# Eight plain feed-forward tiles for six, the factor and modulation sums moved beside them, and a last stage that begins on six output tiles

## The chip, the cores and the metric

The kernel runs on one core of a Trainium2 chip. The metric is the device time in microseconds. Before the change three runs gave 1978.41, 1980.34 and 1980.6, median 1980.34.

## The reference

One layer of a streaming encoder, for 1024 prompt frames and 64 sample frames (1088 tokens in all), model width 1024. Only the last third of the kernel is changed; it computes this:

```
mod = (silu(c) @ w_ada + b_ada).reshape(B, 6, D_MODEL)
sh_m, sc_m, gt_m, sh_f, sc_f, gt_f = (mod[:, j] for j in range(6))
...
u = _rmsnorm(x, g_pre_ffn) * (1.0 + sc_f) + sh_f
f = (jax.nn.silu(u @ w_ffn_gate) * (u @ w_ffn_up)) @ w_ffn_down
x = x + gt_f * _rmsnorm(f, g_post_ffn)
```

The hidden width is 2816, that is 22 tiles of 128 features. `gt_f`, the last sixth of `mod`, is needed only at the very end.

## The kernel before, in words

Every product is done in float32r with each operand split into a high and a low part, so that one product becomes three matmuls (high times high, low weight times high, high weight times low). Weights come from HBM in pieces of 128x512 on SP's queue; ScalarE rounds a piece to its high part (`wh`, line 159) and VectorE subtracts to get the low part (`wl`, line 163). All matmuls are issued at line 132.

The order of the work on each engine is fixed when the program is built. A small model of the machine (`Sched`) keeps a clock per engine; side jobs are Python generators that are resumed between matmuls when the modelled time has come, and what they issue then lands at that place in each engine's queue. Within one engine the order stays as issued.

The feed-forward part has three stages.

1. Plain tiles (`f_tile`): for a feature tile, gate and up products over three chunks of 364, 364 and 360 tokens, each product 24 matmuls into one of three PSUM banks of the tag `d`. ScalarE applies silu to the gate bank, VectorE multiplies by the up bank and forms the low part (tile `hst`), and the result is stored to `d_h` in HBM by a DMA on POOL's queue. Here `NPLAIN` = 6 tiles.
2. Pairs (`gu_pair`): the other 16 tiles are taken two at a time, with Winograd's form of Strassen's method: 7 half-size products (`STEPS`) in place of 8, for gate and then up, and for two halves of the tokens, p = 0 and p = 1, of 2x272 tokens each. A pair is 2x7x2 groups of 12 matmuls of 272 columns. The token side enters as itself (`b11`, `b21`, `b22`) and as four sums `t1` to `t4`, the right factors (`rh`, `rl`), which `right_factors(p)` forms on VectorE and ScalarE, one k index after another. The weight sums (`ws`) are formed on VectorE in scratch slots. Results are gathered in `g[p]`. At the end of a pair `store` takes the high part `hh`, subtracts it from `g[p]` in place, and sends both to `d_h` with two DMAs; the next pair's first gate step writes `g[p]` again.
3. Down (`down_order`): 8 output tiles for three chunks of 416, 416 and 256 tokens; operands `ho` come back from `d_h`. The first chunk begins with three output tiles side by side, so that the weights and operands are taken k range by k range; the others go one tile at a time. `y_chain` then normalises, multiplies by `gt_f` times the gain (`ggf`) and adds the residual.

`ada_rest(3)` forms `gt_f`: 16 loads of 128x512 of `w_ada` on POOL's queue into two halves of one slot, two VectorE accumulations each (`adac`, lines 167 and 172), then a few float32 matmuls into `ps_ms`. It is spawned when the last stage begins. `right_factors(0)` is spawned with the sixth plain job, `right_factors(1)` after it.

Large tiles live in an arena of 39 slots that are handed out first in, first out.

Of the kernel before, what the change touches and what calls it, by code (L numbers as in the profile page):

```python
# [11 lines left out]
F32 = mybir.dt.float32  # L12
F32R = mybir.dt.float32r
AF = mybir.ActivationFunctionType
OP = mybir.AluOpType
# [19 lines left out]
YCH = [(0, 416), (416, 832), (832, T)]  # L35
YSEG = [[(0, 416, 0)], [(0, 416, 0)], [(0, TP - 832, 0), (TP - 832, T - 832, 1)]]
NF = DFF // P
NPLAIN = 6
DNK = [(0, 4), (4, 8), (8, 12), (12, 16), (16, 20), (20, 22)]
HALF = 272  # L40
PAIRS = (0, 2 * HALF)
# [188 lines left out]
def f32(ap):  # L230
    return ap.bitcast(F32)
# [3 lines left out]
def hybrid_step(ctx: ExitStack, tc: tile.TileContext, io):  # L235
    nc = tc.nc
    S = Sched(nc)
# [6 lines left out]
    A = Arena(arena_pool, NSLOT)  # L244
# [5 lines left out]
    def ps(tag, cols=512):  # L250
        cnt[0] += 1
        return psum.tile([P, cols], F32, name=f"ps_{tag}{cnt[0]}", tag=tag, bufs=CAP[tag])
# [42 lines left out]
    class Stream:  # L295
# [37 lines left out]
        def source(self, kind, r, m):  # L333

            if kind is None:
                t, tm = self.raw[r]
                return t[:, 0:m], tm, 1
            (a11, t0), (a21, t1), (a12, t2), (a22, t3) = self.raw[r:r + 4]
            a11, a21, a12, a22 = (x[:, 0:m] for x in (a11, a21, a12, a22))
            if self.sums is None:  # L340
                two = [A.get("ws", F32, [2, 512]) for _ in range(2)]
                self.sum_slots = two
                self.sums = [two[i // 2][:, i % 2, :] for i in range(4)]
            s1, s2, s3, s4 = (x[:, 0:m] for x in self.sums)
            if kind == "11":
                return a11, t0, 0
            if kind == "12":
                return a12, t2, 0
            if kind == "22":
                return a22, t3, 1  # L350
            if kind == "s1":
                return s1, S.tt(s1, a21, a22, OP.add, after=max(t1, t3)), 0
            if kind == "s2":
                return s2, S.tt(s2, s1, a11, OP.add), 0
            if kind == "s3":
                return s3, S.tt(s3, a21, a11, OP.add), 2
            return s4, S.tt(s4, s2, a12, OP.add, after=t2), 1
# [60 lines left out]
    W = Stream()  # L418
# [31 lines left out]
    def down_order(c):  # L450

        if c == 0:
            yield from (((0, 1, 2), a, b) for a, b in DNK)
        for m in range(0 if c else 3, 8):
            yield from (((m,), a, b) for a, b in DNK)

    plain_jobs = [(0, (0,)), (1, (0,)), (0, (1,)), (1, (1,)), (2, (0, 1)), (3, (0, 1)), (0, (2,)), (1, (2,)), (2, (2,)),
# [381 lines left out]
    for c, (c0, c1) in enumerate(CH):  # L839
        for i in range(2):  # L840
            p = kps[i, c]
            n = c1 - c0 if c < 2 else 296
            t = S.now + 0.1
# [61 lines left out]
    for tt in range(9):  # L905
# [4 lines left out]
        p = ps(("po", "ms", "d")[min(tt, 2)])  # L910
        a, m = (tt * P, P) if tt < 8 else (TP, TS)
# [11 lines left out]
        t = S.now + 0.1  # L923
        f = S.act(vs[s][0:m, r, :], p[0:m, 0:256], AF.Copy, after=t)
# [197 lines left out]
    for kind, j in order_a2:  # L1122
        w = W.use()
        if kind == "q":
            q2 = [A.get("q", F32R) for _ in range(2)]
            for c0, c1 in CH:
                p = dense(w, u, c0, c1)
                n = c1 - c0
# [410 lines left out]
    def right_factors(p):  # L1539

        b0 = PAIRS[p]
        rec = A.get("rec", F32, [2, 2 * HALF])
        tf = A.get("tf", F32, [4, HALF])

        def calm():
            while S.t["dve"] > S.now + 0.3:
                yield max(S.now + 0.1, S.t["dve"] - 0.2)

        for i in range(4):
            while len(A.free) < 5:  # L1550
                yield S.now + 0.5
            hi, lo = A.get("rh", F32R, [4, HALF]), A.get("rl", F32R, [4, HALF])
            yield from calm()
            for j, k in enumerate((i, i + 4)):
                S.tt(rec[:, j, :], f32(u2[k][0][:, b0:b0 + 2 * HALF]), f32(u2[k][1][:, b0:b0 + 2 * HALF]), OP.add)
            b11, b12, b21, b22 = (rec[:, j, h * HALF:(h + 1) * HALF] for j in range(2) for h in range(2))
            t1, t2, t3, t4 = (tf[:, j, :] for j in range(4))
            yield from calm()
            S.tt(t1, b11, b12, OP.subtract)
            S.stt(t2, t1, -1.0, b22, OP.mult, OP.subtract)  # L1560
            S.tt(t3, b22, b12, OP.subtract)
            f = S.stt(t4, t2, -1.0, b21, OP.mult, OP.subtract)
            f = S.act(hi[:, :, :], tf[:, :, :], AF.Copy, after=f)
            yield f
            yield from calm()
            S.tt(lo[:, :, :], tf[:, :, :], f32(hi[:, :, :]), OP.subtract, after=f)
            right[p][i] = (hi, lo)
        rec.free()
        tf.free()

    def factor(p, i, name):

        b0 = PAIRS[p]
        if name[0] == "b":
            k = i + 4 * (name[1] == "2")
            h = int(name[2]) - 1
            return tuple(u2[k][l][:, b0 + h * HALF:b0 + (h + 1) * HALF] for l in range(2))
        j = int(name[1]) - 1
        return tuple(right[p][i][l][:, j, :] for l in range(2))
# [23 lines left out]
    def gu_pair(q, g):  # L1603
        hh = {}

        def partial(v, step, o):

            t = S.now + 0.1
            j = (2, 1, 3)[step]
            S.act(v[:, j, :], o, AF.Copy, after=t, scale=-1.0 if step == 1 else 1.0)  # L1610

        def total(v, step, o):
            j, op = ((2, OP.add), (1, OP.subtract), (3, OP.add))[step - 3]
            return j, S.tt(v[:, j, :], v[:, j, :], o, op, after=S.now + 0.1)

        def gate(p, step, o):
            if step == 0 and p in waiting:
                waiting.pop(p)()
            if step < 3:
                partial(g[p], step, o)  # L1620
            elif step < 6:
                j, f = total(g[p], step, o)
                if step == 5:
                    S.act(g[p][:, 1:4, :], g[p][:, 1:4, :], AF.Silu, after=f)
            else:
                S.act(g[p][:, 0, :], o, AF.Silu, after=S.now + 0.1, scale=-1.0)

        def up(p, step, o):
            if step == 0:
                hh[p] = A.get("hh", F32R, [4, HALF])  # L1630
            v = f32(hh[p][:, :, :])
            if step < 3:
                partial(v, step, o)
            elif step < 6:
                j, f = total(v, step, o)
                S.tt(g[p][:, j, :], g[p][:, j, :], v[:, j, :], OP.mult)
            else:
                f = S.stt(g[p][:, 0, :], o, -1.0, g[p][:, 0, :], OP.mult, OP.mult, after=S.now + 0.1)
                f = S.act(hh[p][:, :, :], g[p][:, :, :], AF.Copy, after=f)
                S.spawn(out(p, hh[p], f), at=S.now + 0.3)  # L1640

        def out(p, hi, f):
            finish = waiting[p] = lambda: store(p, hi, f)
            yield f
            if waiting.get(p) is finish:
                waiting.pop(p)
                finish()

        def store(p, hi, f):
            b0 = PAIRS[p]  # L1650
            f2 = S.tt(g[p][:, :, :], g[p][:, :, :], f32(hi[:, :, :]), OP.subtract, after=f)
            for l, src, t in ((0, f32(hi[:, :, :]), f), (1, g[p][:, :, :], f2)):
                S.dma(QP, d_h[2 * q:2 * q + 2, l, :, b0:b0 + 2 * HALF].rearrange("f p t -> p f t"),
                      src.rearrange("p (f h) t -> p f (h t)", f=2), after=t)
            hi.free()
            stored.append(q)

        pair_product(gate)
        pair_product(up)
# [92 lines left out]
    for n, (f, cs_) in enumerate(plain_jobs):  # L1752
        for c in cs_:
            S.idle_until(chains[c])
        f_tile(f, cs_)
        if n == 5:
            factors = S.spawn(right_factors(0))

    def second_factors():
        while not factors[0]:  # L1760
            yield S.now + 0.2
        yield from right_factors(1)

    S.idle_until(S.spawn(second_factors()))
    g = [A.get("g", F32, [4, HALF]) for _ in range(2)]
    for q in range(NPLAIN // 2, NF // 2):
        gu_pair(q, g)
# [23 lines left out]
                op_slots[c, i + m - 1] = sl  # L1791

    for s in (*(s for pair in u2 for s in pair), *(s for p in range(2) for pair in right[p].values() for s in pair), *g,
              *W.sum_slots):
        s.free()
    S.spawn(op_load())

# [21 lines left out]
        sl = f_slots[c] = [A.get("fo", F32, [per, n]) for _ in range(8 // per)]  # L1819
        f_out[c] = lambda m: sl[m // per][:, m % per, :]  # L1820

    ada_last = S.spawn(ada_rest(3))
    for c in range(3):
        n = YCH[c][1] - YCH[c][0]
        begin_out(c)
        banks = {}
        for ms, a, b in down_order(c):
            for m in ms:
                if a == 0:
                    banks[m] = ps("d")  # L1830
                down(banks[m], W.use(), c, a, b, m == 7)
                W.done()
                if b == NF:
                    f_t[c].append(evac(f_out[c](m), banks[m][:, 0:n]))
            if b == NF and len(f_t[c]) in (1, 3) and len(y_done) == c:
                S.idle_until(ada_last)
                y_done.append(S.spawn(y_chain(c)))
    S.idle_all()

# [64 lines left out]
```

## Time and profile before

| | us |
|---|---|
| median of three runs | 1980.34 |
| the profiled execution | 1980.64 |
| its span on the core | 1978.9 |
| TensorE busy | 1864.7 (94%) |
| VectorE busy | 1125.2 (57%) |
| ScalarE busy | 892.3 (45%) |
| POOL busy | 235.9 (12%) |

The mean granted TensorE clock is 0.976 of full speed. The span is what the engines' records cover; the time of the execution is 1.7 us longer. Matmuls overlap each other by their fill and drain, so one lasts longer in the records than the distance to the next; distances between starts are the safer measure, and the idle time ahead of an instruction, with what ended it, tells where TensorE waited. Plain tiles run to 1249.5 us of the span, pairs to 1650.0, the last stage to the end.

### The profile page before, as it was taken

How to read it: one execution, taken by the hardware profiler on the slowest of the kernel's cores; microseconds unless marked ns; L12 is line 12 of the kernel's file. 1: busy time of each engine (PE TensorE's matmuls, PEld its weight loads, DVE VectorE, ACT ScalarE, POOL GpSimd, SP SyncE). 2: the span in 40 equal slices, each digit the busy share in tenths (PEclk: the TensorE clock that was granted, in tenths of full speed). 3: DMA queues.
4: the chain of work that ended last, by engine and by line, in shares of the span. 5: the costliest groups of instructions: out<-in, count | busy, mean ns of one | idle time of the engine just before them, and what ended most of it. 6: DMA issues, size and time to landing. Idle time of an engine off the chain costs nothing.

```text
span 1978.9 us, 32784 instructions
## 1 busy us (share of the span) xinstructions
PE 1864.7 (94%) x12664; PEld 1785.7 (90%) x12664; DVE 1125.2 (57%) x2390; ACT 892.3 (45%) x1854; POOL 235.9 (12%) x387
## 2 busy tenths in 40 slices
PE   7999999999999999999999999699999999299997
PEld 5988888889999999999999999699999989299997
DVE  5555555556877773227758875555555554534454
ACT  5655555555666773212256553233333333143444
POOL 0011111121100001100012111000000003303020
PEclk9999999999999999999999999799999999699998
DMA  8222121233434357644446543122222229559464
GB/s 311 65 67 66 68 67 62 78 112 121 160 127 145 124 174 265 254 146 148 158 158 196 178 149 111 45 88 88 89 88 99 94 89 331 168 151 368 128 220 131
DMA packets 115148, 281.18 MB, mean 142 GB/s; under 512 B 14800, under 2 KB 24272, under 8 KB 114992
## 3 DMA queue, kind: packets, MB, share of 16 engines
q1 hardware_dynamic: 78912, 151.52, 24.0%
q0 software_dynamic: 36080, 127.57, 17.7%
q8 instruction: 99, 1.62, 0.3%
q14 instruction: 57, 0.47, 0.1%
HBM read 210.46 MB, written 68.57 MB: 141 GB/s over the span
## 4 chain that ended last, share of the span: by engine, by line
PE 60%; issue 28%; DMA 7%; DVE 2%; POOL 2%; ACT 1%; SPq 0%; POOLq 0%; DVEq 0%; ACTq 0%
PE ps_d L132 50%; PE ps_sc L132 4%; PE ps_po L132 2%; DMA ada<-w_ada 2%; PE ps_pt L141 2%; DMA ho<-d_h 1%; POOL d_h L186 1%; DMA aol<-d_ao 1%; DMA wr<-w 1%; DVE wl L163 1%; DMA d_h<-g 1%; PE ps_pt L132 1%; ACT kh L159 1%; PE ps_ms L132 0%; DMA x<-xT 0%
## 5 line engine op out<-in xcount | busy, mean ns | idle before, releaser
L163 DVE TENSOR_TENSOR wl<-wr,wh 128x512 fp32r<-128x512 f32 (+2 forms) x424 | 277.8, 675 | 289.6 <-ACT wh L159 289.0
L159 ACT ACTIVATE wh<-wr 128x512 fp32r<-128x512 f32 (+2 forms) x424 | 252.6, 610 | 265.8 <-PE ps_d L132 173.3
L132 PE MATMUL ps_d<-uh,wh 128*128 128x364 f32 (+1 forms) x1080 | 358.8, 332 | 1.5 <-ACT uh L159 1.5
L132 PE MATMUL ps_d<-ul,wh 128*128 128x364 f32 (+1 forms) x1080 | 358.6, 332 | 0.5 <-DVE ul L167 0.5
L132 PE MATMUL ps_d<-uh,wl 128*128 128x364 f32 (+1 forms) x1080 | 358.0, 331 | 0.0
L132 PE MATMUL ps_d<-ho,wh 128*128 128x416 f32 (+1 forms) x1056 | 256.0, 330 | 3.5 <-ACT wh L159 1.9
L132 PEld LDWEIGHTS ps_d<-uh,wh 128*128 128x128 f32 x1080 | 202.8, 188 | 5.7 <-ACT uh L159 1.8
L132 PEld LDWEIGHTS ps_d<-ul,wh 128*128 128x128 f32 x1080 | 203.0, 188 | 4.7 <-DVE ul L167 0.8
L132 PEld LDWEIGHTS ps_d<-uh,wl 128*128 128x128 f32 x1080 | 203.0, 188 | 3.1 <-issue 0.6
L132 PEld LDWEIGHTS ps_d<-ho,wh 128*128 128x128 f32 x1056 | 186.6, 189 | 6.7 <-ACT wh L159 2.3
L132 PE MATMUL ps_d<-ho,wl 128*128 128x416 f32 (+1 forms) x528 | 173.8, 329 | 1.1 <-DVE wl L163 1.0
L132 PE MATMUL ps_d<-u2l,wh 128*128 128x364 f32 (+2 forms) x480 | 150.4, 313 | 0.0
L132 PE MATMUL ps_d<-u2h,wl 128*128 128x364 f32 (+2 forms) x480 | 149.9, 312 | 0.0
L132 PE MATMUL ps_d<-u2h,wh 128*128 128x364 f32 (+2 forms) x480 | 149.8, 312 | 0.0
L132 PEld LDWEIGHTS ps_d<-ho,wl 128*128 128x128 f32 x528 | 99.6, 189 | 2.8 <-DVE wl L163 1.9
L132 PE MATMUL ps_d<-rh,wh 128*128 128x272 f32 x256 | 77.7, 303 | 23.2 <-ACT g L159 23.2
L167 DVE SCALAR_TENSOR_TENSOR adac<-ada,cs,adac 128x512 f32<-128x512 f32 x112 | 78.2, 748 | 34.8 <-DMA ada<-w_ada 34.6
L132 PE MATMUL ps_sc<-rh,wh 128*128 128x272 f32 x256 | 78.0, 305 | 19.3 <-ACT rh L159 15.3
L132 PEld LDWEIGHTS ps_d<-u2h,wh 128*128 128x128 f32 x480 | 90.5, 189 | 0.1
L132 PEld LDWEIGHTS ps_d<-u2h,wl 128*128 128x128 f32 x480 | 90.3, 188 | 0.3
L132 PEld LDWEIGHTS ps_d<-u2l,wh 128*128 128x128 f32 x480 | 90.3, 188 | 0.0
L163 DVE TENSOR_TENSOR wl<-ws,wh 128x512 fp32r<-128x512 f32 x64 | 44.3, 693 | 68.7 <-ACT wh L159 67.6
(343 smaller groups left out, 4156.6 us busy)
## 6 DMA issues: line engine op xcount, KB each, us to landing
wr<-w SPq DMA_DIRECT2D x268, 256.0 KB, 3.2
wr<-w_dn SPq DMA_DIRECT2D x120, 256.0 KB, 3.1
ho<-d_h POOLq DMA_DIRECT2D x44, 416.0 KB, 8.7
gl<-d_ga POOLq DMA_DIRECT2D x16, 544.0 KB, 10.3
d_h<-hh POOLq DMA_DIRECT2D x16, 544.0 KB, 4.1
d_h<-g POOLq DMA_DIRECT2D x16, 544.0 KB, 4.8
ada<-w_ada SPq DMA_DIRECT2D x16, 512.0 KB, 9.6
d_ao<-ohl POOLq DMA_DIRECT2D x64, 128.0 KB, 2.0
```

The costliest lines, as they stand in the source:

```text
L132: self.nc.tensor.matmul(out, lhsT=w, rhs=x, start=start, stop=stop, skip_group_check=part)
L141: self.nc.tensor.transpose(out, in_, ident)
L159: self.nc.scalar.activation(out, in_, func, bias=bias, scale=scale, **kw)
L163: self.nc.vector.tensor_tensor(out, a, b, op=op)
L167: self.nc.vector.scalar_tensor_tensor(out, in0=a, scalar=s, in1=b, op0=op0, op1=op1)
L186: eng.dma_start(out=out, in_=in_)
```

## The change

Two more tiles are done plainly (8), so that seven pairs remain of eight. Both halves' right factors and `gt_f`'s sums become one chain of side jobs, spawned with the first plain job. `store` writes the low part to a slot of its own, `hl`. The four weight sums share two halves of one slot. The first chunk of the last stage begins with six output tiles, in three banks of `d`, two of `sc` and one of `pt`.

```diff
-NPLAIN = 6
+NPLAIN = 8
...
-                two = [A.get("ws", F32, [2, 512]) for _ in range(2)]
-                self.sum_slots = two
-                self.sums = [two[i // 2][:, i % 2, :] for i in range(4)]
+                self.sum_slot = A.get("ws", F32, [2, 512])
+                self.sums = [self.sum_slot[:, i, :] for i in (0, 1, 0, 1)]
...
         if c == 0:
-            yield from (((0, 1, 2), a, b) for a, b in DNK)
-        for m in range(0 if c else 3, 8):
+            yield from ((tuple(range(6)), a, b) for a, b in DNK)
+        for m in range(0 if c else 6, 8):
...
+    def all_factors():
+        for p in range(2):
+            while not chains[p + 1][0]:
+                yield S.now + 0.3
+            yield from right_factors(p)
+        yield from ada_rest(3)
...
-            f2 = S.tt(g[p][:, :, :], g[p][:, :, :], f32(hi[:, :, :]), OP.subtract, after=f)
-            for l, src, t in ((0, f32(hi[:, :, :]), f), (1, g[p][:, :, :], f2)):
+            lo = A.get("hl", F32, [4, HALF])
+            f2 = S.tt(lo[:, :, :], g[p][:, :, :], f32(hi[:, :, :]), OP.subtract, after=f)
+            for l, src, t in ((0, f32(hi[:, :, :]), f), (1, lo[:, :, :], f2)):
...
-        if n == 5:
-            factors = S.spawn(right_factors(0))
-    def second_factors():
-        while not factors[0]:
-            yield S.now + 0.2
-        yield from right_factors(1)
-    S.idle_until(S.spawn(second_factors()))
+        if n == 0:
+            factors = S.spawn(all_factors())
+    S.idle_until(factors)
...
-    ada_last = S.spawn(ada_rest(3))
...
-                    banks[m] = ps("d")
+                    banks[m] = ps("d" if len(ms) == 1 or m < 3 else ("pt" if m == 5 else "sc"))
...
-            if b == NF and len(f_t[c]) in (1, 3) and len(y_done) == c:
-                S.idle_until(ada_last)
+            if b == NF and len(y_done) == c:
```

TensorE's queue in the kernel before, where the sums of `w_ada` (`adac`) are folded: after the last k range of the three output tiles (`ps_d<-ho`) of the last stage.

```order
9777 L132 MATMUL ps_d_16734<-ho_16711,wh_16917 128x416
9778 L132 MATMUL ps_d_16734<-ho_16711,wl_16918 128x416
9779 L132 MATMUL ps_d_16734<-ho_16713,wh_16917 128x416
9780 L132 MATMUL ps_ms_17062<-adac_16682,one_82 32x256 x4
9781 L132 MATMUL ps_ms_17062<-adac_16683,one_82 32x256 x4
9782 L141 MATMUL ps_ms_17062<-ident,adac_16682 128x128 x2
9783 L132 MATMUL ps_d_17078<-ho_16642,wh_16935 128x416
```

The same matmuls in the changed kernel stand within the last product of the last plain tile (`ps_d<-u2h`), just ahead of the first pair (272 columns).

```order
7178 L132 MATMUL ps_d_13233<-u2l_10864,wh_13046 128x360
7179 L132 MATMUL ps_d_13233<-u2h_10865,wh_13046 128x360
7180 L132 MATMUL ps_ms_13265<-adac_12765,one_82 32x256 x4
7181 L132 MATMUL ps_ms_13265<-adac_12766,one_82 32x256 x4
7182 L132 MATMUL ps_d_13233<-u2h_10865,wl_13047 128x360
7183 L132 MATMUL ps_d_13233<-u2l_10866,wh_13046 128x360
7184 L141 MATMUL ps_ms_13265<-ident,adac_12765 128x128 x2
7185 L132 MATMUL ps_d_13298<-u2h_10851,wh_13082 128x272
```

So the fold has moved ahead by the whole stage of pairs and the first three output tiles.

VectorE's queue before, where the accumulation begins: behind the copy of an output tile (`fo`) of the last stage out of its bank.

```order
2003 L163 TENSOR_TENSOR wl_16998<-wr_16939,wh_16997 128x512
2004 L178 COPY fo_16638<-ps_d_16734 128x416
2005 L163 TENSOR_TENSOR wl_17009<-wr_16957,wh_17008 128x256
2006 L172 TENSOR_SCALAR adac_16682<-ada_16684,cs 128x512
2007 L172 TENSOR_SCALAR adac_16683<-ada_16684,cs 128x512
2008 L172 TENSOR_SCALAR adac_16682<-ada_16684,cs 128x512
2009 L172 TENSOR_SCALAR adac_16683<-ada_16684,cs 128x512
2010 L167 SCALAR_TENSOR_TENSOR adac_16682<-ada_16684,cs,adac_16682 128x512
```

In the changed kernel the accumulations stand between the two steps that finish each chunk of a plain tile (`hst`).

```order
1641 L163 TENSOR_TENSOR wl_12870<-wr_12648,wh_12869 128x512
1642 L167 SCALAR_TENSOR_TENSOR adac_12766<-ada_12767,cs,adac_12766 128x512
1643 L167 SCALAR_TENSOR_TENSOR adac_12765<-ada_12767,cs,adac_12765 128x512
1644 L167 SCALAR_TENSOR_TENSOR adac_12766<-ada_12767,cs,adac_12766 128x512
1645 L167 SCALAR_TENSOR_TENSOR adac_12765<-ada_12767,cs,adac_12765 128x512
1646 L167 SCALAR_TENSOR_TENSOR adac_12766<-ada_12767,cs,adac_12766 128x512
1647 L163 TENSOR_TENSOR hst_12895<-hst_12895,ps_d_12897 128x364
1648 L163 TENSOR_TENSOR hst_12895<-hst_12895 128x364
1649 L167 SCALAR_TENSOR_TENSOR adac_12765<-ada_12767,cs,adac_12765 128x512
```

Five accumulations stand ahead of this chunk's two `hst` steps, and eight between them and the next chunk's.

## Rows read from the trace of the kernel before

**Rows 1.** The page's 40 slices: TensorE's busy tenths and granted clock.

```profile
PE   7999999999999999999999999699999999299997
...
PEclk9999999999999999999999999799999999699998
```

**Rows 2.** TensorE's waits from 1250 to 1730: total us, times, longest.

```profile
PE ps_ms L132 <- DVE adac L167: 35.8, 2, 35.1
PE ps_d L132 <- ACT g L159: 23.2, 7, 4.8
PE ps_sc L132 <- ACT rh L159: 15.3, 4, 5.3
```

**Rows 3.** TensorE's timeline, plain tiles into first pair: start, us, instruction.

```profile
1201.76 0.33 PE L132 MATMUL ps_d<-u2h,wh 128*128 128x364 f32 x1
...
1249.51 0.29 PE L132 MATMUL ps_d<-u2h,wh 128*128 128x272 f32 x1
...
1282.30 0.29 PE L132 MATMUL ps_d<-u2h,wh 128*128 128x272 f32 x1
```

**Rows 4.** The same timeline, first change of pair, and the last stage's first matmul.

```profile
1318.44 0.29 PE L132 MATMUL ps_d<-rh,wh 128*128 128x272 f32 x1
...
1319.94 0.29 PE L132 MATMUL ps_sc<-rh,wh 128*128 128x272 f32 x1
...
1324.68 0.39 PE L132 MATMUL ps_d<-rh,wh 128*128 128x272 f32 x1 [3.07 <-ACT g L159]
...
1650.04 0.35 PE L132 MATMUL ps_d<-ho,wh 128*128 128x416 f32 x1
```

**Rows 5.** Timeline of DVE, POOL and ACT at the first change of pair.

```profile
1319.26 2.49 DVE L163 TENSOR_TENSOR g<-g,hh 128x1088 f32<-128x1088 f32 x2
...
1320.85 0.73 POOL L186 DMA_DIRECT2D d_h<-g  x1 [2.72 <-DVE g L163]
...
1324.23 0.40 ACT L159 ACTIVATE g<-ps_d 128x272 f32<-128x272 f32 x1 [5.62 <-DMA d_h<-g]
```

**Rows 6.** TensorE's timeline in the last stage, around the `adac` matmuls.

```profile
1687.50 0.34 PE L132 MATMUL ps_d<-ho,wh 128*128 128x416 f32 x1
1722.91 1.07 PE L132 MATMUL ps_ms<-adac,one 128*32 128x256 f32 x4 [35.07 <-DVE adac L167]
...
1727.47 0.69 PE L132 MATMUL ps_d<-ho,wh 128*128 128x416 f32 x1
```

**Rows 7.** Windows: length, busy us (instructions) of PE, PEld, DVE, ACT, POOL; clock, DMA.

```profile
1201.70:1249.50 47.80, 47.80 (x290) 47.80 (x289) 19.27 (x34) 12.17 (x22) 4.36 (x6) 1.00 0.22 77
1249.50:1282.30 32.80, 15.45 (x74) 13.03 (x74) 21.88 (x37) 8.90 (x14) 0.73 (x1) 0.64 0.14 44
...
1604.80:1616.90 12.10, 7.33 (x39) 6.91 (x38) 3.23 (x4) 2.69 (x7) 2.17 (x3) 0.72 0.44 166
1650.00:1687.80 37.80, 37.80 (x200) 36.90 (x198) 13.64 (x20) 12.87 (x22) 12.57 (x18) 1.00 0.95 355
```

**Rows 8.** Tile `ada` from 1640 to 1730 (durations min/median/max), two loads in POOL's timeline.

```profile
L167 DVE SCALAR_TENSOR_TENSOR adac<-ada,cs,adac x28: 744/747/753, 1693.7 to 1724.6; 128x512 f32<-128x512 f32 x28
L186 POOL DMA_DIRECT2D ada<-w_ada x16: 539/539/609, 1660.8 to 1720.8; - x16
...
1709.56 0.54 POOL L186 DMA_DIRECT2D ada<-w_ada  x1 [2.49 <-DVE adac L167]
...
1714.28 0.54 POOL L186 DMA_DIRECT2D ada<-w_ada  x1 [2.38 <-DVE adac L167]
```

**Rows 9.** Groups of 1225.3 to 1249.5, the last plain tile: count, busy us, mean ns, idle before.

```profile
L163 DVE TENSOR_TENSOR hst<-hst 128x364 f32<-128x364 f32 (+1 forms) x3 | 1.6, 536 | 1.7 <-ACT hst L159 1.7
L163 DVE TENSOR_TENSOR hst<-hst,ps_d 128x364 f32<-128x364 f32 (+1 forms) x3 | 1.6, 532 | 11.7 <-PE ps_d L132 11.7
```

**Rows 10.** POOL's timeline, loads of the last stage's operands.

```profile
1631.68 3.62 POOL L186 DMA_DIRECT2D ho<-d_h  x5 [22.06 <-PE ps_sc L132]
1646.23 7.22 POOL L186 DMA_DIRECT2D ho<-d_h  x10 [10.93 <-PE ps_sc L132]
```

More of the change, by code (lines that the diff above doesn't have):

```diff
@@ L1655, in store @@
             hi.free()
+            lo.free()
             stored.append(q)
@@ L1793, in hybrid_step @@
     for s in (*(s for pair in u2 for s in pair), *(s for p in range(2) for pair in right[p].values() for s in pair), *g,
-              *W.sum_slots):
+              W.sum_slot):
         s.free()
```

## Prediction

> **What bounds the kernel now.** I read the page's slices first. TensorE is at nine tenths or more nearly everywhere and dips at two places, the slices with 6 (about 1240 to 1290 us) and with 2 (about 1680 to 1730), and the granted clock dips there too [rows 1]. So TensorE is the bound, and a change gains by what it takes out of its queue or out of its idle time. Next came TensorE's waits from 1250 on [rows 2]: 35.8 us for `adac` on VectorE, 15.3 us for the right factors `rh`, and 23.2 us, in seven waits, for ScalarE's write of `g`. These are the three things that the change touches. The timeline of TensorE then gave the lengths, and the windows the clock that goes with them.
>
> Distances between starts are the unit. From 1282.30 to 1318.44 [rows 3, 4] TensorE runs 24 groups of 12 matmuls of 272 columns with no wait (the first pair's seventh group to the second pair's third): 1.506 us a group, so 42.16 us for a pair's 28 groups. Two plain tiles, 288 matmuls, run from 1201.76 to 1249.51 [rows 3]: 47.75 us.
>
> **The pairs.** The stage runs from 1249.51 to 1650.04 [rows 3, 4], 400.53 us. Eight pairs without waits would be 8 x 42.16 = 337.3. The other 63.2 us are waits and slow clock, in two parts.
>
> Right factors: the first six groups took 1282.30 - 1249.51 = 32.79 us for 9.04 of work, an excess of 23.8. There TensorE follows the second half's factors as VectorE makes them, and the mean granted clock is 0.64 [rows 7]. In the changed kernel these factors are finished among the plain tiles, so the whole excess goes.
>
> Changes of pair: the remaining 39.4 us lie in seven changes, 5.6 each. At the first one, the group that began at 1319.94 is the last before the wait, which lasts until 1324.68 [rows 4]. ScalarE's write to `g` waits for the DMA that reads `g` [rows 5]: the subtraction was done in place, so the store has to leave first. With `hl` the write has to wait only for the subtraction. Two subtractions take 2.49 us from 1319.26 [rows 5], so the first half's is through at about 1320.5, ScalarE's write of 0.40 at 1320.9. TensorE wants the bank at 1324.68 - 3.07 = 1321.6. The margin is 0.7 us, so I take no wait; what ends last is then TensorE itself. Bounds: 0, and 1 us at each of six changes if the margin is lost. The second excess, the slow clock after the wait, goes with it: at the last change 12.1 us pass for three groups, 4.5 of work, at a clock of 0.72 [rows 7].
>
> The eighth pair itself goes as well (-42.2), and two plain tiles come (+47.75): that swap alone costs 5.6 us. Stage of pairs and tiles together: -63.2 - 42.2 + 47.75 = -57.6.
>
> **The sums for the last stage.** TensorE's last `ho` matmul before the wait starts at 1687.50, the next at 1727.47 [rows 6]; with 0.19 us for the first (198 matmuls between 1650.04 and there) the gap is 39.8 us. It goes, and the fold, the few matmuls on `adac`, comes back ahead of the pairs. In the gap they took 1727.47 - 1722.91 = 4.6 us with waits at about half clock [rows 6]; half of that without waits is under 2. Bounds 1.7 and 4.6, I take 2. The clock is lost nowhere else by this.
>
> What covers the moved work? 32 accumulations of 0.75 us at most [rows 8], 24 us, and four more factor steps, under 21.9 us (all of VectorE's work in that window) [rows 7], stand now beside plain tiles. Two tiles load VectorE with 19.3 of 47.8 us [rows 7], so eight have room for both. The finer question is order, since VectorE's queue waits for loads of `w_ada`. A chunk takes TensorE 47.75 / 6 = 7.96 us. VectorE needs for its two `hst` steps 0.53 + 0.54 and some 0.57 between them [rows 9], 1.6 us. Two loads turn round in 1714.28 - 1709.56 = 4.7 us [rows 8], that is four accumulations. In the order the chunks get 7, 5, 8, 7, 3 and 2 accumulations ahead of them; eight take 9.4, so VectorE may fall behind by 3.1 us there, by 1 before and 3 after: 7.3 us in all if nothing overlaps, and then recovers. A chunk's up bank is asked for again three products on, that is after two products, 7.96 us. So even the worst count costs nothing, though barely; loads in flight during the `hst` steps make it smaller. I take 0. TensorE's fold stands two chunks behind the last accumulation.
>
> A rule speaks against this. POOL took 539 ns for nearly each load of `ada`, 609 at most, with VectorE at work beside it [rows 8]: no blocking is seen. The Trainium skill (SBUF — State Buffer, "SBUF: two separate sides") says that while VectorE runs an instruction in a two-port mode, POOL is locked out of the port they share and cannot write the descriptors of a DMA from its queue. If the accumulations counted as such, each load could wait for one of 0.75 us, two in each turn of two loads; over the five turns in question the lag would be 7.5 us more, 14.8 against 7.96, and TensorE would wait some 7 us, about 10 with the slow clock (the last change of pair lost 2.8 us beside its wait of 4.8 [rows 2, 7]). By the row the term is 0, and I go by the row.
>
> The first factor step now stands ahead of the third chunk's `u2`, which plain tiles wait for. The trace doesn't show how much that chain can slip. From the four steps in 21.9 us [rows 7] a step is at most 5.5 us; bounds 0 and 5.5, and as VectorE has gaps there I take 1.
>
> **The last stage on six tiles.** The same matmuls in another order. Before, the stage began with 37.80 us busy of 37.80 at DMA 0.95 [rows 7], so there is no wait to win. With six tiles a range of four k lasts 72 x 0.19 = 13.7 us in place of 6.8, so operands are wanted half as fast. Their loads are issued as slots come free, 15 of them by 1653 [rows 10], and in the new order 20 stand ahead of the last stores on POOL's queue; the last two pieces, which wait for these stores, are wanted only 68 us after the start. The banks of `sc` and `pt` are wanted 6.8 us after it, when the last pair has been read. I take 0, with up to 10 us above if operands and weights crowd each other at that DMA load. The shared scratch slot of the weight sums costs nothing: the third sum writes where the first stood, and the first's split is earlier on VectorE itself. The slot for `hl` was last read a pair earlier.
>
> **The sum.** -57.6 - 39.8 + 2 + 1 = -94.4. From the execution's own 1980.64 (0.3 above the median of the runs, 1.7 above its span) that gives 1886 us, 4.8% faster.
>
> **Rivals.**
> VectorE's lag reaches TensorE: it becomes the bound in the accumulation stretch. For it: the worst count uses up 7.3 of 7.96 us. Against: VectorE under 65% of the stage. Price, worked out from a lag of up to twice the worst count: a stall of up to 7 us with 3 of slow clock, once or twice, so 1896 to 1906. The Trainium skill's rule on the shared port (SBUF — State Buffer) would bring the same rival about, at 1896.
> The change of pair keeps a wait, that of ScalarE behind VectorE: for it, a margin of 0.7 us; against it, that the queue orders on both engines stand as they did and only the DMA's part goes. If half the excess stays, 6 x 2.8 = 17 us: 1903. If the store's wait stays entirely (the change does not do what it says), 34 us: 1920.
> The last stage waits for operands: 15 POOL loads and the weights already fill the DMA engines to 0.95. Up to 20 us with slow clock: 1906.
> Slower than before: VectorE so late that most chunks of the plain tiles stall. One stall costs as the last change of pair did, 12.1 - 4.5 = 7.6 us. It decides from 94.4 / 7.6, 13 of the 24 chunks; at 16 chunks, those beside the factors and sums, it is +122 and the time 2008. Against it: VectorE's load in those rows, and no wait of TensorE in 47.80 us of two tiles [rows 7].
>
> **How the numbers follow.** Forecast 0.70, its own range 1880 to 1896 (six changes at 1 us, the fold at 4.6; below, 0.3% for what one run differs from another). VectorE's lag 0.11, change of pair 0.09, last stage 0.06, slower 0.04. The range from 1880 to 1904 takes in the forecast and the milder half of the next three cases; outside are their worse half, the slower case and a twentieth below, 2 in 10 together. 0.2% is what a measurement here can tell from no change. All cases but the last lie far below 1976, so faster 0.96; of the last 0.01 goes to a loss that just cancels the gain (same) and 0.03 to slower.
>
> **What would show it.** In the changed profile TensorE should wait nowhere over 1 us between 1110 us and the middle of the last stage; a pair should repeat every 42.2 us; the stage of pairs should last 295 us; the wait for `adac` should be gone and no `d_h<-g` exist; the clock should read 1.00 through pairs and the first 100 us of the last stage. Waits of `ps_d` for `hst` during the accumulations would show the first rival, waits for `g` at each 42nd us the second, waits for `ho` or `wh` just after the pairs the third. The forecast is wrong if two plain tiles with accumulations among them take over 52 us, or if the changes of pair cost over 2 us each.

## The result and the profile after

The changed kernel takes 1891.42 us (median of four runs, 1888.79 to 1893.09); the kernel before, beside it, 1980.47. The ratio is 0.955, 95% interval 0.9533 to 0.9567. The forecast was 1886 us, within 1880 to 1904. The profiled execution of the changed kernel took 1893.09 us with a span of 1891.2.

The page's slices of the changed kernel, TensorE and its clock, answer to [rows 1]:

```profile
PE   7999999999999999999999999999999999999997
...
PEclk9999999999999999999999999999999999999998
```

Both dips are gone, and with them the dips of the clock. TensorE's waits from 1250 to 1730 us (total us, times, longest) answer to [rows 2]:

```profile
PE ps_d L132 <- DVE g L163: 2.5, 3, 1.5
PE ps_d L132 <- DMA ho<-d_h: 1.9, 3, 0.9
```

None of the three waits of [rows 2], 74.3 us in all, is left. What the first line shows is a new, small wait within the pairs; the second was there before too (1.7 us in three waits), only later, past 1800 us.

TensorE's timeline of the changed kernel (start, us, instruction): the first matmul of the plain tiles, the fold of the sums and the first pair, the first matmul of the last stage. It answers to [rows 3] and to the last row of [rows 4].

```profile
1106.52 0.33 PE L132 MATMUL ps_d<-u2h,wh 128*128 128x364 f32 x1
...
1301.75 1.07 PE L132 MATMUL ps_ms<-adac,one 128*32 128x256 f32 x16
...
1303.33 0.44 PE L141 MATMUL ps_ms<-ident,adac 128*128 128x128 f32 x2
1303.52 0.37 PE L132 MATMUL ps_d<-u2h,wh 128*128 128x272 f32 x1
...
1603.04 0.36 PE L132 MATMUL ps_d<-ho,wh 128*128 128x416 f32 x1
```

With these starts the two profiles can be laid side by side. The kernel before began its plain tiles at 1101.77, and up to there TensorE has the same instructions in the same order in both.

| stretch | before | after | difference | forecast |
|---|---|---|---|---|
| start to the plain tiles | 1101.77 | 1106.52 | +4.75 | 0 |
| plain tiles | 147.74 | 197.00 | +49.3 | +50.75 |
| pairs | 400.53 | 299.52 | -101.0 | -105.4 |
| last stage, to the end of the span | 328.86 | 288.16 | -40.7 | -39.8 |
| sum | 1978.9 | 1891.2 | -87.7 | -94.4 |

Windows of the changed kernel (length, busy us of PE, PEld, DVE, ACT, POOL with instructions, clock, DMA share, GB/s): two plain tiles with the accumulations, one pair, the beginning of the last stage. They answer to [rows 7].

```profile
1254.20:1302.00 47.80, 47.80 (x294) 47.49 (x295) 31.37 (x50) 9.81 (x20) 10.86 (x18) 1.00 0.43 144
1394.00:1436.00 42.00, 42.00 (x335) 41.88 (x334) 24.08 (x44) 16.63 (x32) 2.90 (x4) 1.00 0.31 101
1603.00:1700.00 97.00, 97.00 (x515) 96.02 (x514) 36.66 (x57) 38.10 (x68) 25.62 (x36) 1.00 0.75 266
```

TensorE is busy all the time in each, at a clock of 1.00. In the first, VectorE has 31.4 us to do in place of 19.3, and TensorE doesn't wait for it.

The first change of pair, which answers to [rows 5]: VectorE's subtraction into `hl`, POOL's stores, ScalarE's writes of `g`, and TensorE's group that asks for the bank.

```profile
1349.68 2.48 DVE L163 TENSOR_TENSOR hl<-g,hh 128x1088 f32<-128x1088 f32 x2
```

```profile
1351.27 0.72 POOL L186 DMA_DIRECT2D d_h<-hl  x1 [2.72 <-DVE hl L163]
1351.99 0.72 POOL L186 DMA_DIRECT2D d_h<-hh  x1
```

```profile
1351.08 0.40 ACT L159 ACTIVATE g<-ps_d 128x272 f32<-128x272 f32 x1 [2.04 <-DVE hl L163]
1352.28 0.40 ACT L159 ACTIVATE g<-ps_sc 128x272 f32<-128x272 f32 x1 [0.80 <-DVE hl L163]
```

```profile
1351.89 0.29 PE L132 MATMUL ps_d<-rh,wh 128*128 128x272 f32 x1
```

ScalarE's first write now waits for `hl`, no longer for the DMA, and starts 0.2 us before the store is even issued. It ends at 1351.48; TensorE takes the bank at 1351.89 without a wait. The margin is 0.4 us.

The small wait that the pairs have instead: VectorE in the first half of the second pair, and TensorE behind it.

```profile
1360.42 0.69 DVE L163 TENSOR_TENSOR ws<-wr,wr 128x512 f32<-128x512 f32 x1 [5.40 <-DMA wr<-w]
...
1365.16 0.43 DVE L163 TENSOR_TENSOR g<-g,ps_d 128x272 f32<-128x272 f32 x1
```

```profile
1365.65 0.39 PE L132 MATMUL ps_d<-rh,wh 128*128 128x272 f32 x1 [1.54 <-DVE g L163]
```

VectorE sits for 5.4 us on a sum of weights whose pieces have not landed; the additions to `g`, which free TensorE's banks, stand behind it in its queue. TensorE loses 1.5 us two links further on. VectorE's wait itself is older than the change. Its line over the pairs without the late factors (1282 to 1650) in the kernel before, and in the run below that changes the store alone (1282 to 1616):

```profile
DVE ws L163 <- DMA wr<-w: 12.0, 7, 2.1
```

```profile
DVE ws L163 <- DMA wr<-w: 24.1, 7, 4.1
```

The changed kernel has 25.1 us in seven such waits; with its store in place again (the first run below) it has 11.4. So the waits double where the pairs no longer stand still for the store. The run with 24.1 keeps two scratch slots for the weight sums, so the shared slot isn't the reason.

### The profile page after: what moved, and what is told of

Its sections match the earlier page's. It is cut to its first block, busy times and chain, and to the rows that moved or that the text cites. A ratio compares the mean times of both kernels' runs of the same rounds, so it can differ in the third digit from the quotient of the medians.

```text
span 1891.2 us, 32607 instructions
## 1 busy us (share of the span) xinstructions
PE 1855.7 (98%) x12616; PEld 1782.8 (94%) x12616; DVE 1110.8 (59%) x2366; ACT 883.7 (47%) x1842; POOL 236.9 (13%) x389
## 4 chain that ended last, share of the span: by engine, by line
PE 80%; DMA 7%; issue 6%; DVE 4%; ACT 2%; POOL 1%; SPq 0%; POOLq 0%; ACTq 0%; DVEq 0%
PE ps_d L132 64%; PE ps_sc L132 9%; PE ps_po L132 2%; PE ps_pt L141 2%; DMA ho<-d_h 2%; PE ps_pt L132 2%; DMA ada<-w_ada 1%; DMA aol<-d_ao 1%; DVE wl L163 1%; DMA wr<-w 1%; ACT wh L159 1%; DMA d_h<-hl 1%; ACT kh L159 1%; DMA xre<-d_x 1%; DVE g L163 0%
## 5 line engine op out<-in xcount | busy, mean ns | idle before, releaser
L132 PE MATMUL ps_d<-ho,wh 128*128 128x416 f32 (+1 forms) x924 | 220.8, 326 | 2.7 <-DMA ho<-d_h 1.9
L132 PE MATMUL ps_d<-u2l,wh 128*128 128x364 f32 (+2 forms) x552 | 174.9, 317 | 0.0
L132 PE MATMUL ps_d<-u2h,wl 128*128 128x364 f32 (+2 forms) x552 | 174.7, 316 | 0.0
L132 PE MATMUL ps_d<-u2h,wh 128*128 128x364 f32 (+2 forms) x552 | 174.3, 316 | 0.0
L132 PEld LDWEIGHTS ps_d<-ho,wh 128*128 128x128 f32 x924 | 162.2, 189 | 5.5 <-DMA ho<-d_h 2.3
L132 PE MATMUL ps_d<-ho,wl 128*128 128x416 f32 (+1 forms) x462 | 150.8, 326 | 0.9 <-DVE wl L163 0.9
L132 PEld LDWEIGHTS ps_d<-u2h,wl 128*128 128x128 f32 x552 | 103.9, 188 | 0.8 <-issue 0.4
L159 ACT ACTIVATE pts<-ps_pt 128x512 f32<-128x512 f32 (+2 forms) x80 | 40.0, 511 | 95.7 <-PE ps_pt L141 95.5
L159 ACT ACTIVATE wh<-ws 128x512 fp32r<-128x512 f32 x56 | 35.1, 627 | 96.0 <-DVE ws L163 96.0
L159 ACT ACTIVATE s<-s,stt_s 128x256 f32<-128x256 f32 (+1 forms) x144 | 69.7, 484 | 16.2 <-DVE stt_s L995 16.0
```

The source lines that it names most:

```text
L132: self.nc.tensor.matmul(out, lhsT=w, rhs=x, start=start, stop=stop, skip_group_check=part)
L159: self.nc.scalar.activation(out, in_, func, bias=bias, scale=scale, **kw)
```

## Experiments

The store undone alone (in place again, everything else as changed):

```diff
-            lo = A.get("hl", F32, [4, HALF])
-            f2 = S.tt(lo[:, :, :], g[p][:, :, :], f32(hi[:, :, :]), OP.subtract, after=f)
-            for l, src, t in ((0, f32(hi[:, :, :]), f), (1, lo[:, :, :], f2)):
+            f2 = S.tt(g[p][:, :, :], g[p][:, :, :], f32(hi[:, :, :]), OP.subtract, after=f)
+            for l, src, t in ((0, f32(hi[:, :, :]), f), (1, g[p][:, :, :], f2)):
...
-            lo.free()
```

> The changed kernel (1891.4 us) with the old store: the subtraction in place in g, no slot of its own for the low part. Theory (each of the three waits is separate and costs what it cost before): the wait for the DMA that reads g comes back at six changes of pair, 5.6 us each with the slow clock after it, +34 us: 1925. Rival (the wait was long before only because other stalls put the pair boundary beside other transfers): under +20 us, below 1912. Seen in the trace: ps_d waits for ACT g of about 3 us, six times.

Measured: 1923.47 us, ratio 0.9701 (0.9683 to 0.9719), 32 us above the changed kernel. TensorE's waits from 1250 to 1730:

```profile
PE ps_d L132 <- ACT g L159: 18.3, 6, 3.1
PE ps_sc L132 <- ACT g L159: 4.6, 4, 3.6
```

Six waits for six changes of pair are back, behind the DMA that reads `g`. They sum to 22.9 us, and the time is 32 us longer. The stage of pairs in the windows:

```profile
1301.45:1632.96 331.51, 308.59 (x2355) 305.50 (x2355) 170.97 (x310) 118.65 (x225) 26.29 (x37) 0.96 0.30 99
```

It is 32.0 us longer than in the changed kernel. TensorE is busy for 308.6 us of it with what is 7 x 42.16 = 295.1 us of work without waits, at a mean granted clock of 0.96: what the waits leave goes to the slow clock around them.

The store alone (the kernel before, with `hl`):

> The kernel before (1980.5 us) with nothing changed but the low part's own slot. Theory: the seven changes of pair lose their 39.4 us of wait and slow clock: 1941; the waits for factors and for the sums stay as they are. Rival (the gain needs the other parts too, since the weights' loads and VectorE are as far behind as TensorE): a new wait takes half of it or more, above 1960.

Measured: 1947.44 us, ratio 0.9825 (0.9808 to 0.9842), 34.6 us below the kernel before in that set. Its first pair, its last stage, and TensorE's waits in the pairs behind the factors:

```profile
1249.14 0.29 PE L132 MATMUL ps_d<-u2h,wh 128*128 128x272 f32 x1
...
1616.39 0.35 PE L132 MATMUL ps_d<-ho,wh 128*128 128x416 f32 x1
```

```profile
PE ps_d L132 <- DVE g L163: 1.9, 4, 0.8
PE ps_sc L132 <- ACT g L159: 1.5, 2, 1.2
```

The pairs take 367.25 us in place of 400.53. Less the factors' excess of 23.8 and 337.3 us of work, 6.1 us are left, of which 3.4 are these waits on `g`. So the separate low part is worth 32 to 35 us whichever way it is taken: 32 for six changes of pair when it is undone, 33.3 (by the trace) or 34.6 (by the medians) for seven when it stands alone; the forecast had 39.4 for the seven.

The sums late (changed kernel, `ada_rest(3)` spawned at the last stage again):

```diff
-        yield from ada_rest(3)
...
+    ada_last = S.spawn(ada_rest(3))
...
             if b == NF and len(y_done) == c:
+                S.idle_until(ada_last)
```

> The changed kernel with the sums for the last gate spawned at the last stage again (factors still among the plain tiles, six tiles at the start of the last stage). Theory: the gap of 39.8 us comes back less the fold of 1.5 to 2 that leaves the plain stage: +38, 1929. Rival (with six tiles the first k ranges last twice as long, so that the loads and accumulations are covered by them): +10 or less, under 1902; or in between if VectorE gets to them only after the tiles' copies.

Measured: 1908.9 us, ratio 0.963 (0.9612 to 0.9648), 17.5 us above the changed kernel: neither the theory nor its rival, but the case in between that the expectation left open. TensorE around the fold:

```profile
1676.27 0.55 PE L132 MATMUL ps_pt<-ho,wh 128*128 128x416 f32 x1
1689.45 1.07 PE L132 MATMUL ps_ms<-adac,one 128*32 128x256 f32 x4 [12.63 <-DVE adac L167]
```

The wait for `adac` is there, but 12.6 us long where [rows 6] has 35.1. Six output tiles put the fold 80 us behind the stage's start (1596.34 to 1676.27), three put it 37.5 behind. The accumulations, and another wait of TensorE in the last stage:

```profile
L167 DVE SCALAR_TENSOR_TENSOR adac<-ada,cs,adac x28: 744/748/753, 1652.0 to 1690.8; 128x512 f32<-128x512 f32 x28
...
L172 DVE TENSOR_SCALAR adac<-ada,cs x4: 478/478/480, 1647.8 to 1649.0; 128x512 f32<-128x512 f32 x4
```

```profile
PE ps_pt L132 <- DVE wl L163: 3.4, 1, 3.4
```

The sums came later too: the last accumulation starts 94 us after the stage's start (1690.8 - 1596.3), in the kernel before 75 (1724.6 - 1650.0, [rows 6, 8]). VectorE's queue reaches the first one after 51 us (1647.8 - 1596.3), behind splits of weights rather than the tiles' copies, and more splits stand between the accumulations. TensorE in turn waits once for such a split (`wl`).

Three output tiles at the start of the last stage (changed kernel otherwise):

```diff
-            yield from ((tuple(range(6)), a, b) for a, b in DNK)
+            yield from ((tuple(range(3)), a, b) for a, b in DNK)
-        for m in range(0 if c else 6, 8):
+        for m in range(0 if c else 3, 8):
```

> The changed kernel with three output tiles at the start of the last stage in place of six. Theory (the last stage had no wait for operands to win): no change, 1890 to 1893. Rival (six tiles give the operand loads time that they need): +5 us or more, 1897, with waits of ps_d for ho or wh after the pairs.

Measured: 1888.49 us, ratio 0.9534 (0.9513 to 0.9555): no difference that the intervals show. Both together, late sums and three tiles, were run to see whether the two edits stand in for each other:

> The changed kernel with both of these undone: the modulation sums are spawned at the last stage again, and that stage begins on three output tiles. With six tiles, late sums cost 17.5 us; with the sums early, three tiles cost nothing. Theory A (the two edits overlap: either six tiles or early sums give TensorE the time in which the sums run, and only early sums give all of it): the whole gap of the kernel before is back, 39.8 less the fold's 1 us, about 1927 us, and TensorE waits for adac for 33 to 37 us. Theory B (the edits are independent, six tiles cover nothing): the same 17.5 as with six tiles, 1906 us.

Measured: 1927.55 us, ratio 0.9723 (0.9709 to 0.9736); TensorE waits 36.0 us for `adac`:

```profile
PE ps_ms L132 <- DVE adac L167: 36.0, 2, 35.3
```

That makes a square of four:

| | sums early | sums late |
|---|---|---|
| six output tiles | 1891.4 | 1908.9 |
| three output tiles | 1888.5 | 1927.6 |

With the sums late, six tiles are worth 18.7 us; with the sums early, nothing that can be told from the noise. The two edits overlap, and the early sums alone do the whole work.

Six plain tiles (changed kernel otherwise):

```diff
-NPLAIN = 8
+NPLAIN = 6
```

> The changed kernel with six plain tiles, as before the change, and eight pairs. Theory A (six tiles have room enough beside them for the factors and sums; two plain tiles for one pair cost 47.75 - 42.2 = 5.6 us and nothing else): 1891.4 - 5.6 = 1886 us, 1884 to 1888. Theory B (the two more tiles are what gives VectorE and the loads of w_ada the time): a wait of the first pair for the last factors or of TensorE for adac, the clock below 1.00 there, 1900 us or more.

Measured: 1922.07 us, ratio 0.9696 (0.9682 to 0.9709), 30.7 us slower than with eight. Theory A fell, and of theory B it is the wait for `adac` that came. TensorE's wait for the sums, the fold in its timeline, and the windows of the six tiles and of what follows:

```profile
PE ps_ms L132 <- DVE adac L167: 35.5, 2, 33.5
```

```profile
1283.93 1.06 PE L132 MATMUL ps_ms<-adac,one 128*32 128x256 f32 x4 [33.47 <-DVE adac L167]
```

```profile
1102.60:1250.00 147.40, 147.40 (x928) 146.36 (x928) 117.43 (x235) 70.30 (x130) 20.05 (x31) 1.00 0.43 144
1250.00:1289.70 39.70, 3.76 (x21) 1.21 (x21) 23.04 (x34) 2.14 (x4) 7.19 (x13) 0.53 0.35 109
```

The gap for `adac` has only moved, from the last stage to the end of the plain tiles. The sums follow the factors in one chain. Tile `ada` in the changed kernel and in the one with six tiles (durations min/median/max, first and last start; of the second the loads on POOL alone):

```profile
L167 DVE SCALAR_TENSOR_TENSOR adac<-ada,cs,adac x28: 743/748/755, 1253.8 to 1293.1; 128x512 f32<-128x512 f32 x28
L186 POOL DMA_DIRECT2D ada<-w_ada x16: 537/539/659, 1241.3 to 1289.4; - x16
```

```profile
L186 POOL DMA_DIRECT2D ada<-w_ada x16: 537/537/659, 1240.0 to 1283.2; - x16
```

In both the first load is issued some 135 us after the plain tiles begin (1241.3 - 1106.5; 1240.0 - 1102.6), about when the factors are done, and the sums take 43 to 48 us of loads from there. Six tiles end at 147 us; eight end at 197, with the last accumulation at 187 (1293.1 - 1106.5).

Ten plain tiles:

```diff
-NPLAIN = 8
+NPLAIN = 10
```

> The changed kernel with ten plain tiles and six pairs. Theory A (swap price): one more swap, +5.6 us, 1897 us; with a pair in the trace at 42.5 rather than 42.16 us, +5.2. Theory B (more plain tiles loosen something that still binds): 1892 us or less.

Measured: 1897.67 us, ratio 0.9572 (0.9559 to 0.9585); by the ratios 0.0022 x 1980 = 4.4 us above eight, by the medians 6.3. Theory A holds within the intervals: once the chain is covered, each swap of a pair for two tiles is a plain loss.

Six plain tiles with the sums late again, which asks whether the factors alone fit beside six:

```diff
-NPLAIN = 8
+NPLAIN = 6
...
-        yield from ada_rest(3)
...
+    ada_last = S.spawn(ada_rest(3))
...
             if b == NF and len(y_done) == c:
+                S.idle_until(ada_last)
```

> The changed kernel with six plain tiles, the factors still beside them, and the modulation sums at the last stage again. Theory A (six tiles hold the factors; only the sums did not fit there): the kernel with late sums and eight tiles took 1908.9 us, one swap of 5.6 us less makes 1903 us, and no wait for rh or rl in the first pair. Theory B (six tiles don't hold the factors either, their excess of 23.8 us comes back in part): 1912 us or more.

Measured: 1905.75 us, ratio 0.9605 (0.9583 to 0.9627). Against 0.963 with eight tiles this is 5 us less, near the swap's price; the intervals overlap, but the traces agree: plain tiles and pairs together take 488.9 us (1105.86 to 1594.75) in place of 493.8 (1102.56 to 1596.34). No wait for `rh` or `rl` is left in its pairs. The factors fit beside six tiles; only the sums behind them don't.

Six plain tiles with factors and sums as two jobs at once:

```diff
-NPLAIN = 8
+NPLAIN = 6
...
-        yield from ada_rest(3)
...
+            ada_last = S.spawn(ada_rest(3))
             factors = S.spawn(all_factors())
     S.idle_until(factors)
+    S.idle_until(ada_last)
```

> The changed kernel with six plain tiles, factors and modulation sums as two side jobs at once, not one after the other. Theory A (VectorE has room beside six tiles, the chain of one job behind the other was only too long): the wait of 33.5 us for adac shrinks to under 5, 1886 to 1893 us. Theory B (VectorE and the turn-round of the loads are full up to the end of six tiles, whatever the order; in its queue 14 accumulations still stand in a row after the last tile's first chunks): a wait of 10 to 25 us stays, 1900 to 1915 us.

Measured: 1909.97 us, ratio 0.9627 (0.9604 to 0.965). Its waits from the plain tiles on:

```profile
PE ps_ms L132 <- DVE adac L167: 21.6, 2, 19.8
```

Theory B: a wait of 21.6 us stays. The last accumulation starts 172 us after the plain tiles begin (1273.4 - 1101.8), in place of 184 in the chain (1286.8 - 1102.6). Two jobs at once win 12 us, and six tiles are still too short. Other orders in VectorE's queue were not tried.

More raw weight pieces in flight, for the small wait that was left in the pairs:

```diff
-        RAW, LIVE = 4, 6
+        RAW, LIVE = 6, 5
```

> The changed kernel with six buffers for raw weight pieces in place of four, and five for split ones in place of six (there is no room for more). Theory A (the waits for g left in the pairs, 2.5 us at three places and about 4.4 us of the stage with their slow starts, come from weight pieces that land late, because only four are in flight; two more start earlier): these waits go, 2 to 4 us less, 1888 us. Theory B (the loads collide with the stores whatever the depth, or a fifth split buffer less costs as much): 1891 us or more, with the waits for g still in the trace.

Measured: 1899.32 us, ratio 0.9582 (0.9569 to 0.9595), slower by 6 to 8 us. It won time in one place and lost it in another. Windows over the stage of pairs of the changed kernel and of this one, and what TensorE has in this one at 900 us:

```profile
1303.52:1603.04 299.52, 297.02 (x2355) 296.03 (x2354) 170.33 (x310) 116.97 (x225) 26.23 (x37) 1.00 0.34 110
```

```profile
1313.01:1607.94 294.93, 294.93 (x2353) 294.93 (x2353) 171.50 (x307) 118.74 (x226) 26.21 (x37) 1.00 0.33 111
```

```profile
899.12 0.67 PE L132 MATMUL ps_d<-roh,wh 128*128 128x364 f32 x1 [4.97 <-ACT wh L159]
```

The stage of pairs is without a single wait now, at the length that was forecast (295.1), while a place well ahead of it pays. In both kernels ScalarE stands still there for 19 to 20 us behind VectorE (`gl`); with six split pieces in stock TensorE comes through it without a wait, with five it doesn't. The first plain tile starts at 1111.6, 5 us later than in the changed kernel, and the tiles take 201.4 us in place of 197.0. So pairs and the rest were taken apart: one pool of 16 buffers, six raw and ten split in the pairs, four and twelve elsewhere.

```diff
...
-            while self.i_load < (upto or len(self.raws)) and self.i_load - self.i_free < self.RAW:
+            while self.i_load < (upto or len(self.raws)) and self.i_load - self.i_free < (
+                    6 if self.i_load in self.pair_raws else self.RAW) and self.bufs:
...
+            if kind and self.i_split - self.i_done >= 5 or not keep and len(self.bufs) < 2:
+                return False
...
```

> The changed kernel with the 16 weight buffers as one pool: in the pairs six hold raw pieces and ten split ones (5 pieces), elsewhere four and twelve as now. With six and five throughout, the stage of pairs fell from 299.5 to 294.9 us and its waits for g went, but TensorE waited 5.0 us for wh at about 900 us, well ahead of the stages changed here. Theory A (both come from the depth alone): the pairs keep the gain and nothing is lost elsewhere, 1891.4 - 4.6 = 1887 us, 1885 to 1889. Theory B (the gain in the pairs came of the later start of that run): 1891 us and the waits for g are back.

Measured: 1887.79 us, ratio 0.9513 (0.9494 to 0.9531); this is below the changed kernel by 3.6 us of the medians and 0.0037 x 1980 = 7 us of the ratios, and the two intervals just fail to touch. Its stage of pairs in the windows, to be read against the one above:

```profile
1305.85:1601.52 295.67, 295.67 (x2353) 295.67 (x2353) 171.66 (x307) 119.15 (x226) 26.28 (x37) 1.00 0.33 109
```

3.85 us less in the stage, with no wait of TensorE in it, and no wait at 900. VectorE's waits in the pairs of the changed kernel have this line, which is missing in those of this one:

```profile
DVE ws L163 <- DMA wr<-w: 25.1, 7, 5.4
```

So the seven waits, one in each pair, come from the depth of the loads. What the depth is worth in time is less sure. The median is the lowest here, but the interval overlaps that of the run with three output tiles (1888.49 us). And in this execution the plain tiles take 200.5 us (1105.31 to 1305.85) in place of 197.0, which gives back 3.5 of the 3.85 us; the mean clock from 1140 to 1180 is 0.96, and TensorE has this wait there:

```profile
PE ps_ms L132 <- DVE nb L163: 2.0, 1, 2.0
```

The same wait is 0.2 us long with ten tiles and 0.8 with two jobs at once, and absent in the changed kernel. Whether it belongs to the edit stays open.

## Why the prediction held, point by point

**Factors, -23.8.** Right by the trace: the first pair starts without a wait (1303.52), its stretch has TensorE busy throughout, and six tiles already cover the factors. No run undoes this term alone; with the store alone changed, the waits for `rh` stand unchanged at 15.3 us.

**Changes of pair, -39.4.** The mechanism was right, the size 4 to 6 us too large, and one sign of it was missed: no wait over 1 us was to be seen, and one of 1.5 is there. The wait for the store went at every change, as the in-place run shows from the other side. The margin, put at 0.7 us, was 0.4. What the step missed is what is late next: I had looked for it on ScalarE behind the subtraction, and it was VectorE behind a load of weights, 14 us after the change of pair. That wait stood in the kernel before as well (12.0 us in all), where TensorE was held by the store and did not feel it. Four pieces in flight are just one group of four, so a delayed load is felt at once. The term measured -35.0 in the changed kernel (4.4 us left of 39.4) and -33.3 with `hl` alone; with six pieces in flight it reaches the forecast.

**Eighth pair and two tiles, +5.6.** The price was right: 5 us between six and eight tiles with late sums, 4.4 between eight and ten. What the prediction did not see is what the price buys. It entered the two tiles as a loss and said that eight tiles have room for the sums; it did not ask whether six have. They don't: without them the gap of the sums comes back as 33.5 us at the end of the plain tiles. The slack in the changed kernel is small too. The last accumulation starts at 1293.1 and the tiles end at 1303.5. The prediction added up VectorE's work and never the length of the chain, and it put VectorE under 65% of the stage; it was busy for 147.8 of 197.0 us, 75%. That eight tiles cover the chain, by 10 us, was partly luck.

**The gap for `adac`, -39.8, and the fold, +2.** Right: -40.7 in the last stage. The fold took 1.5 us, just below the bounds of 1.7 to 4.6: the eight tiles last 197.0 us with it and 195.5 in the runs with late sums. Its 16 matmuls with no wait fill one stretch of 1.07 us at full clock, and two transposes come behind. As an attribution the term is the early sums' alone, and it includes the 18.7 us that six tiles would have saved without them (with the sums late, 1927.6 against 1908.9).

**VectorE's lag, 0.** Right: no wait of TensorE for `hst` in the whole plain stage. (The worst count's terms, 3.1, 1 and 3, make 7.1 us and not 7.3; nothing hung on it.) The rule on the shared port, weighed there, has its test here too. POOL's 16 loads took 537 to 659 ns in the changed kernel, the seven that ran while an accumulation did among them, much as in [rows 8], and its stores 0.72 us beside the subtraction into `hl`. The trace shows none of the blocking that the Trainium skill (SBUF — State Buffer, "SBUF: two separate sides") describes for VectorE's two-port modes; the runs don't tell which mode these instructions take.

**The chain ahead of the plain tiles, +1.** The plain stage came out 1.5 us shorter than forecast: of the 3 us put in for fold and chain, the fold took 1.5. Nothing of this term can be seen.

**Six output tiles, 0.** Right, shown by the run with three.

**What the sum lacks.** 94.4 was forecast, 87.7 measured between the two profiles, 89 between the medians. Of the 6.7 us, 4.4 are the waits for weights in the pairs. 4.75 lie ahead of the first plain tile, where the two kernels have the same order. I take that for run-to-run: in the profiles of this study with the same weight buffers the first plain tile starts between 1101.4 and 1106.5 us, and the changed kernel's profile is the latest of them. The plain tiles and the last stage give 2.4 back.

The rivals: the lag of VectorE and the operands of the last stage show in no wait over 1 us; the pairs kept a remainder of 4 us where half the excess, 17, was feared, and from another wait than the feared one; the slower case did not come near.

## What to carry to other kernels

When several side jobs are strung into a chain, take the length of the chain and of the stretch that must cover it before valuing either: here 187 us against 147 or 197, and a seemingly useless two tiles were worth 31 us. Two edits that feed the same wait should be valued together, since each may be worth all or nothing depending on the other. After a wait is removed, look at the queue of the engine that now ends last for an instruction that waits for a load: everything behind it waits too, and here the depth of the loads decided whether it did.

## What the runs showed of the hardware

The DMA issues of the changed kernel between 1350 and 1366, and then the weight loads between 1306 and 1345 (KB each, median us to land): the one weight load beside three stores of 544 KB on POOL's queue took 6.4 us; ten, with a single store of 360 KB among them, took a median of 3.2. The last line is the next change of pair (1387 to 1401), four loads beside four such stores: the median is only 3.7, so the 6.4 is no rule for every load.

```profile
d_h<-hl POOLq DMA_DIRECT2D x2, 544.0 KB, 4.3
d_h<-hh POOLq DMA_DIRECT2D x1, 544.0 KB, 4.1
wr<-w SPq DMA_DIRECT2D x1, 256.0 KB, 6.4
```

```profile
wr<-w SPq DMA_DIRECT2D x10, 256.0 KB, 3.2
```

```profile
wr<-w SPq DMA_DIRECT2D x4, 256.0 KB, 3.7
```

A wait costs more than its length where the granted clock falls with it: 35.5 us of waiting for `adac` with six plain tiles came with a clock of 0.53 over 39.7 us (the lower level, 1.2 of 2.4 GHz, for nearly all of it, TensorE having stood idle), and the waits of the in-place run sum to 22.9 us where the time was 32 us longer, at a mean clock of 0.96 in its pairs. The small waits of the changed kernel did not bring the clock down: its pairs hold a mean of 1.00 with three waits of 0.2 to 1.5 us among them.
